# Band attention's q and k: from a token-wise projection inside the mixer stage to four units of seven products ahead of it

## The chip, the cores and the metric

One Trainium2 chip, one core in use. The metric is the device time of one execution in microseconds (us), the median over runs; lower is better. Everything is float32: a product of two float32 matrices is made from fp32r parts, each operand split into a high part (a cast) and a low part (what the cast lost), as three matmuls: high by high, high by low, low by high.

## The reference, cut to what matters

One layer of a streaming encoder for 1024 tokens of width 1024. The part that the change touches is the second of two token mixers, attention in a band:

```python
h = rmsnorm(x, norm_mix_g)
qa, fa, ia, ga, qb, kb, vb, gate_a, gate_b = split(h @ w_in)
oa = hgrn2_mixer(qa, fa, ia, ga, ...)            # 4 heads of 128
qh = head_rms(qb.reshape(8 heads, 64), qn_g)     # norm over the 64 features of a head, times a gain
kh = head_rms(kb.reshape(8 heads, 64), kn_g)
scores = qh . kh * 64 ** -0.5 + bias[clipped distance]     # own chunk of 64 and the 8 before it
ob = softmax(scores) . vb
x = x + (sigmoid(gate_a) * (oa @ w_a) + sigmoid(gate_b) * (ob @ w_b)) @ w_out
x = x + SwiGLU(rmsnorm(x));  x = x + sigmoid(rmsnorm(x) @ w_pg) * (p @ w_pe)
```

`head_rms(t, g)` is `t * rsqrt(mean(t * t) + 1e-6) * g`.

## The kernel before, in words

Activations lie feature by feature: a tile has 128 features on the partitions and 1024 tokens along the free axis. The kernel runs through these stages in order.

**Units of seven products** (`units`, L900). The normed input `u` is eight pairs of tiles. After a first stage come ten jobs (`JOBS`), each of which makes two blocks of 128 output features for all 1024 tokens. A job is one call of `strassen` (L1605): the 2 x 2 block product (two feature blocks by two token halves) is made with seven products instead of eight, each product being 4 x 3 matmuls of 128x128 by 128x512, so 84 matmuls a unit. Sums of weight quarters, their casts and low parts are made one unit ahead (`strassen_weights`: DVE sums, ACT casts, POOL and DVE low parts), in steps called `side` between the products. DVE adds products together; each finished quarter (block `c`, token half `half`) goes to a callback `done`. A "gate" or "out" unit's callback, `gate_done` (L888), multiplies by the row of the outer norm (`rb`), applies a sigmoid or silu, and stores the 128x512 result to DRAM. Temporaries of 128x512 come from a pool of eight (`stmp`, tag "tmp"). PSUM has eight banks of 128x512; a unit uses three.

**HGRN mixer** (`hgrn_mix`). Four heads, woven with a filling stream of matmul pieces (`fill`): gates, the projection of v (`attn_v`), and the first four pieces of the next stream, `feed`.

**Attention** (`attention`, L722). 32 steps, each a (pair of heads, block of 128 tokens). `feed` begins with `attn_in` (L609): the q/k projection token by token, in two passes of eight blocks of four pieces (a piece is six matmuls); for each block ACT squares, DVE sums over 64 columns, POOL takes the power -1/2, and DVE scales and doubles the columns. For each step `attn_stack` (L646) transposes four 128x128 blocks on TensorE and writes the stacks to which scores are computed: for q, 64 rows of high part over 64 rows of low part; for k, the high part twice (`k1`) and the low part twice (`k2`), so that two matmuls make a score block. After `attn_in`, `feed` holds the last two gate blocks (`gate`), eight pieces each. Two pieces of `feed` are put into every step.

A step n, in the order in which each engine gets its work: last stage of head 1 of step n-1 (reciprocal and scaling of its probabilities), scores of step n for head 0 and head 1 (matmuls, then on DVE `tensor_tensor_reduce`: add the bias and keep the running minimum of the negated scores), on odd steps the probability-times-v products of the two steps n-3 and n-2, the transposes of step n-1 for head 1 (`attn_pt`, copies by ACT and DVE), exponentials of head 0 and head 1 on ACT with their sums, transposes of step n-1 for head 0, scaling of head 0. A block has 128 to 640 key columns: the first four blocks of a pair have fewer. The steps go through the blocks with two pairs side by side.

The order on TensorE, DVE, ACT, POOL and the DMA queue of SP is pinned: `Pinned` and `order` (L88) chain each instruction to the one before it on its engine, so an engine works in the order of the program. In the profile, L72 is that helper for DVE, ACT and POOL, L102 is `mul`, L105 is `tr`, L97 is `load`; tiles have to be told apart by name (`pm` PSUM, `s` a slot of 128x1024, `m` a small tile of the mixer, `t` a temporary, `whi`/`wlo`/`wh`/`wl` weight parts, `wr` raw weights, `q` weight sums, `d` DRAM).

**The rest.** Branch products, output projection, 22 feed-forward units of seven products, the down projection and the last block. The sums of weight quarters for two of these are made by DMA: `copies` in the mixer, then adding transfers on POOL's queue (`adds`), one every other step of the attention loop, the others later.

Of the kernel before, what the change touches and what calls it, by code (L numbers as in the profile page):

```python
# [10 lines left out]
F32 = mybir.dt.float32  # L11
# [20 lines left out]
FIRST = 4  # L32
RING = 4
# [4 lines left out]
JOBS = (('gate', 6), ('head', 1), ('gate', 8), ('head', 2), ('gate', 10), ('head', 3), ('gate', 12), ('gate', 14), ('out', 0), ('out', 2))  # L38
# [36 lines left out]
class Trunk:  # L75
    def __init__(self, tc, d, out):
# [5 lines left out]
        self.queue, self.calls = None, 0  # L82
        self.by_turns = self.pinned = False
# [162 lines left out]
    def norm_sums(self):  # L246
# [9 lines left out]
        if self.epsv is None:  # L256
            self.epsv = self.small(8, tag="epsv")
            nc.vector.tensor_scalar(self.epsv, v, EPS, None, ALU.mult)
# [12 lines left out]
    def setup(self):  # L271
# [6 lines left out]
        one = cp.tile([P, 3], F32, name="ones")  # L278
        self.ones, self.warm, self.gq8 = [one[:, i:i + 1] for i in range(3)]
        nc.vector.memset(self.ones, 1.0)  # L280
        nc.vector.tensor_copy(self.onesr, self.ones[:, :].to_broadcast([P, P]))
# [3 lines left out]
        nc.vector.tensor_scalar(self.gq8, self.cols[:, C_GQ:C_GQ + 1], 0.125, None, ALU.mult)  # L285

# [136 lines left out]
    def hgrn_mix(self, h):  # L423
# [26 lines left out]
        while m < P:  # L450
# [46 lines left out]
            if m == 16:  # L497
                self.keep_heads(self.oa, self.od, self.done_heads)
            yield 1240
# [14 lines left out]
        if self.oa[h] is None:  # L514
            self.oa[h] = self.slot()
        pks = []
# [87 lines left out]
    def attn_setup(self):  # L604
        self.k1 = [self.slot(F32R) for _ in range(4)]
        self.k2 = [self.slot(F32R, late=i > 1) for i in range(4)]
        self.qs = {}

    def attn_in(self):  # L609

        nc = self.nc
        late = []

        def scale():
            two, b, ps, ss = late.pop(0)
            for i in range(2):
                qk = self.small(HALF, tag="qk")
                self.V.tensor_tensor(
                    qk[:, :].rearrange("p (a two d) -> p a two d", two=2, d=64),
                    ps[:, i * 256:i * 256 + 256].rearrange("p (a d) -> p a d", d=64).unsqueeze(2).to_broadcast([P, 4, 2, 64]),  # L620
                    ss[:, 4 * i:4 * i + 4].unsqueeze(2).unsqueeze(3).to_broadcast([P, 4, 2, 64]), ALU.mult)
                self.qk[2 * two + i, b] = qk

        for two in range(2):
            ws = self.weights(4, ahead=0)
            for b in range(8):
                pss = []
                for n, _ in enumerate(self.tokens(ws, (b,), pss)):
                    if b == 7:
                        self.weights(0, ahead=n + 1 if two == 0 else 2, direct=True)  # L630
                    if n < 3:
                        yield 1296
                    if n == 0 and late:
                        scale()
                (ps,) = pss
                sq = self.small(HALF, tag="sq")
                self.A.activation(sq, ps, AF.Square)
                ss = self.small(8)
                self.V.tensor_reduce(ss, sq[:, :].rearrange("p (a d) -> p a d", d=64), axis=AX.X, op=ALU.add)
                self.V.tensor_scalar(ss, ss, 1.0 / 64, self.epsv[:, b:b + 1], ALU.mult, ALU.add)  # L640
                self.G.tensor_tensor(ss, ss, self.mhalf[:, 0:8], ALU.pow)
                late.append((two, b, ps, ss))
                yield 1296
        self.scale = scale

    def attn_stack(self, pair, b):  # L646

        qk = self.qk.pop((pair, b))
# [1601 lines left out]
```

## Time and profile before

| | before |
|---|---|
| median of 3 runs | 1546.96 us (1546.4 to 1548.36) |
| the profiled execution | 1549.86 us, span 1548.0 us |
| granted TensorE clock | 1.00 |
| TensorE busy | 1520.7 us (98%) |
| VectorE (DVE) busy | 1127.2 us (73%) |
| ScalarE (ACT) busy | 670.7 us (43%) |
| GpSimd (POOL) busy | 626.7 us (40%) |
| one unit of seven products | 19.02 us |
| attention loop, first score matmul to last probability-times-v | 434.6 to 633.5 us |

How to read the lines: a row of a table by stretch gives the stretch, its length, and for each engine busy time with the number of instructions, then the granted clock, the DMA share and the rate. A row of a group gives line, engine, operation, output<-inputs, shapes and count, then busy time and mean duration in ns, then the idle time of that engine just before these instructions and what ended it. A row in order of time gives start, duration, engine, line and operation, and in brackets the idle time before it. PE is TensorE, PEld its weight load. Durations of matmuls overlap, since they are pipelined; from start to start is what one costs in a stream.

### The profile page before, as it was taken

How to read it: one execution, taken by the hardware profiler on the slowest of the kernel's cores; microseconds unless marked ns; L12 is line 12 of the kernel's file. 1: busy time of each engine (PE TensorE's matmuls, PEld its weight loads, DVE VectorE, ACT ScalarE, POOL GpSimd, SP SyncE). 2: the span in 40 equal slices, each digit the busy share in tenths (PEclk: the TensorE clock that was granted, in tenths of full speed). 3: DMA queues.
4: the chain of work that ended last, by engine and by line, in shares of the span. 5: the costliest groups of instructions: out<-in, count | busy, mean ns of one | idle time of the engine just before them, and what ended most of it. 6: DMA issues, size and time to landing. Idle time of an engine off the chain costs nothing.

```text
span 1548.0 us, 20662 instructions
## 1 busy us (share of the span) xinstructions
PE 1520.7 (98%) x7664; PEld 1266.2 (82%) x7664; DVE 1127.2 (73%) x1645; ACT 670.7 (43%) x1136; POOL 626.7 (40%) x349
## 2 busy tenths in 40 slices
PE   8999999999999999999999999999999999999998
PEld 6888888878788888788888788888888888888886
DVE  5787774776777778446888877777777767656678
ACT  6633333433377677421567222222222234456552
POOL 4233333010333222245212656665555545445546
PEclk9999999999999999999999999999999999999999
DMA  5544444898433443767346244443233288785425
GB/s 201 195 164 143 143 150 154 270 325 258 145 82 69 111 75 73 294 178 230 102 158 216 91 119 125 128 124 111 104 110 101 101 303 305 273 282 188 130 96 203
DMA packets 97044, 256.56 MB, mean 166 GB/s; under 512 B 10032, under 2 KB 14896, under 8 KB 96432
## 3 DMA queue, kind: packets, MB, share of 16 engines
q1 hardware_dynamic: 90400, 239.51, 45.0%
q0 software_dynamic: 6400, 15.73, 6.2%
q8 instruction: 60, 0.98, 0.3%
q14 instruction: 40, 0.33, 0.1%
q10 hardware_dynamic: 144, 0.02, 0.0%
HBM read 193.08 MB, written 93.59 MB: 185 GB/s over the span
## 4 chain that ended last, share of the span: by engine, by line
PE 89%; DVE 6%; ACT 2%; DMA 1%; issue 1%; POOL 0%; SPq 0%; DVEq 0%; ACTq 0%; POOLq 0%
PE pm L102 86%; DVE s L72 4%; PE pm L105 3%; DVE m L72 1%; ACT m L72 0%; ACT wh L142 0%; DMA s<-in_x 0%; DMA wr<-in_qk 0%; DMA wr<-in_fm 0%; DVE q L72 0%; ACT s L72 0%; DVE wl L72 0%; DMA wr<-in_wv 0%; DVE s L337 0%; DVE t L72 0%
## 5 line engine op out<-in xcount | busy, mean ns | idle before, releaser
L102 PE MATMUL pm<-s,whi 128*128 128x512 f32 x1792 | 552.4, 389 | 0.6 <-DVE t L72 0.6
L102 PE MATMUL pm<-s,wh 128*128 128x512 f32 (+1 forms) x1584 | 492.5, 392 | 7.0 <-ACT wh L142 5.2
L102 PEld LDWEIGHTS pm<-s,whi 128*128 128x128 f32 x1792 | 336.0, 188 | 71.5 <-DVE t L72 1.7
L102 PEld LDWEIGHTS pm<-s,wh 128*128 128x128 f32 x1584 | 295.6, 188 | 69.9 <-ACT wh L142 5.2
L102 PE MATMUL pm<-s,wlo 128*128 128x512 f32 x896 | 348.6, 389 | 0.0
L72 DVE TENSOR_TENSOR s<-s,s 128x512 f32<-128x512 f32 (+3 forms) x236 | 285.5, 1238 | 61.2 <-ACT s L72 47.7
L102 PE MATMUL pm<-s,wl 128*128 128x512 f32 x792 | 308.7, 390 | 0.5 <-POOL wl L150 0.5
L150 POOL TENSOR_TENSOR wl<-wr,wh 128x1024 fp32r<-128x1024 f32 (+2 forms) x72 | 175.3, 2440 | 222.5 <-ACT wh L142 222.4
L72 DVE TENSOR_TENSOR t<-pm,t 128x512 f32<-128x512 f32 x158 | 108.8, 689 | 132.9 <-PE pm L102 105.6
L142 ACT CAST wh<-wr 128x1024 fp32r<-128x1024 f32 (+2 forms) x106 | 106.5, 1005 | 208.4 <-PE pm L102 92.1
L102 PEld LDWEIGHTS pm<-s,wlo 128*128 128x128 f32 x896 | 168.2, 188 | 34.8
L102 PE MATMUL pm<-wh,s 128*128 128x512 f32 x512 | 180.0, 407 | 0.0
L102 PEld LDWEIGHTS pm<-s,wl 128*128 128x128 f32 x792 | 149.2, 188 | 32.0 <-POOL wl L150 1.2
L72 POOL TENSOR_TENSOR wlo<-wr,whi 128x512 fp32r<-128x512 f32 (+1 forms) x63 | 132.3, 2106 | 68.2 <-ACT whi L72 59.2
L72 POOL TENSOR_TENSOR wlo<-q,whi 128x512 fp32r<-128x512 f32 x62 | 100.0, 1614 | 139.7 <-ACT whi L72 75.5
L72 POOL TENSOR_TENSOR m<-m,mhalf 128x8 f32<-128x8 f32 (+1 forms) x24 | 35.0, 1459 | 229.1 <-DVE m L72 229.1
L72 ACT CAST s<-s 128x1024 fp32r<-128x1024 f32 (+1 forms) x94 | 90.4, 981 | 61.9 <-DVE s L72 31.6
L72 ACT CAST whi<-q 128x512 fp32r<-128x512 f32 (+1 forms) x93 | 70.5, 758 | 107.3 <-PE pm L102 84.6
L102 PEld LDWEIGHTS pm<-wh,s 128*128 128x128 f32 x512 | 96.4, 188 | 18.5
L72 POOL TENSOR_TENSOR s<-t,rb 128x512 f32<-128x512 f32 x44 | 70.7, 1607 | 98.5 <-ACT t L72 96.1
L102 PE MATMUL pm<-wl,s 128*128 128x512 f32 x256 | 99.9, 390 | 0.0
L72 ACT ACTIVATE t<-s 128x512 f32<-128x512 f32 x44 | 27.8, 633 | 159.3 <-DVE s L72 155.3
(147 smaller groups left out, 1835.3 us busy)
## 6 DMA issues: line engine op xcount, KB each, us to landing
s<-d SPq DMA_DIRECT2D x81, 512.0 KB, 6.2
d<-s SPq DMA_DIRECT2D x87, 256.0 KB, 2.4
wr<-d SPq DMA_DIRECT2D x36, 512.0 KB, 3.7
d<-s SPq DMA_DIRECT2D x32, 512.0 KB, 4.4
d<-t SPq DMA_DIRECT2D x46, 256.0 KB, 2.3
wr<-in_sg SPq DMA_DIRECT2D x22, 512.0 KB, 3.9
wr<-in_su SPq DMA_DIRECT2D x22, 512.0 KB, 4.9
s<-in_x SPq DMA_DIRECT2D x21, 512.0 KB, 8.6
```

The costliest lines, as they stand in the source:

```text
L72: return lambda *a, **k: self.trunk.order(op(*a, **k), self.key)
L102: return self.order(self.nc.tensor.matmul(*a, **k))
L105: return self.order(self.nc.tensor.transpose(*a, **k))
L142: self.nc.scalar.copy(hi[:, c], raw[:, c])
L150: rest.tensor_tensor(lo[:, c], raw[:, c], f32(hi[:, c]), ALU.subtract)
```

## The change

- q and k of pair p (128 features each) become the two blocks of a new kind of unit, `("qk", p)`. Four of them are put among the last jobs, so there are fourteen units. Units q/k 0 and 1 stand between gate and out units, 2 and 3 stand side by side, and one out unit follows.
- Their callback `qk_done` works on 128x512: multiply by `rb` (DVE), square (ACT), cast to a high part (ACT), low part (DVE). From then on the rest of the chain is done one step per product (`tick`), beginning two products later: two matmuls with a constant block matrix `blk` (1/64 inside each head's 64 x 64 block) sum over partitions; logarithm with eps as bias, then exponential of -1/2 of it (ACT); multiply (DVE); scale by the gain into a high part (ACT); low part (DVE); store both parts to DRAM (`qkd`).
- The attention stage loads q and k back as stacks: `attn_q` loads for each head 64 rows of the high part over 64 rows of the low part, 512 tokens at a time; `attn_k` loads the high part twice and the low part twice. For the first pair this is asked for in head 3 of the HGRN mixer, for later pairs in blocks 4 and 5 of the pair before, the bias in block 6.
- `attn_in`, `attn_stack`, their eight weight tiles and `epsv` go. `feed` is the two gate blocks alone; three pieces are used ahead of the attention loop, one in each of the steps 4, 8, 12, 16, 20, 24 (`FILL`), the rest after it.
- The steps go through one pair after the other. Score tiles `s` have four buffers instead of three.
- Adding transfers are issued in every fourth step instead of every second one. Heads of the result are stored at other steps.

```diff
-JOBS = (('gate', 6), ('head', 1), ('gate', 8), ('head', 2), ('gate', 10), ('head', 3), ('gate', 12), ('gate', 14), ('out', 0), ('out', 2))
+FILL = (4, 8, 12, 16, 20, 24)
+JOBS = (
+    ('gate', 6), ('head', 1), ('gate', 8), ('head', 2), ('gate', 10), ('head', 3), ('gate', 12), ('qk', 0), ('gate', 14), ('qk', 1),
+    ('out', 0), ('qk', 2), ('qk', 3), ('out', 2))
...
+        nc.vector.tensor_scalar(self.blk, f32(self.onesr[:, :]), 0.0, None, ALU.mult)
+        for r in (slice(0, 64), slice(64, P)):
+            nc.vector.tensor_scalar(self.blk[r, r], f32(self.onesr[r, r]), 1.0 / 64, None, ALU.mult)
...
+    def attn_q(self, p, half):
+        hs = slice(half * HALF, half * HALF + HALF)
+        for h in range(2):
+            q = self.q[p, h, half] = self.small(HALF, F32R, tag="qk")
+            for i in range(2):
+                self.load(f32(q[64 * i:64 * i + 64, :]), self.qkd[p][0][i][64 * h:64 * h + 64, hs])
+
+    def attn_k(self, p, h):
+        self.k[p, h] = [self.slot(F32R) for _ in range(2)]
+        for k, src in zip(self.k[p, h], self.qkd[p][1]):
+            for i in range(2):
+                self.load(f32(k[64 * i:64 * i + 64, :]), src[64 * h:64 * h + 64, :])
...
-        steps = [(2 * two + p, b) for two in range(2) for b in range(8) for p in range(2)]
+        steps = [(p, b) for p in range(4) for b in range(8)]
-        feed = chain(self.feed, self.gate(ahead=3), self.gate(ahead=2))
+        feed = self.feed
...
+        def loads(p, b):
+            if b == 0:
+                self.attn_q(p, 1)
+            if p < 3 and b == 4:
+                self.attn_q(p + 1, 0)
+            if p < 3 and 4 <= b < 6:
+                self.attn_k(p + 1, b - 4)
+            if p < 3 and b == 6:
+                self.attn_bias(p + 1)
...
-            if n % 2 and n < whole:
+            if n % 4 == 1 and n < whole:
                 next(self.adds)
             stage(n - 1, 1)
-            next(feed, None)
+            if n in FILL:
+                next(feed, None)
             if n < whole:
...
                 scores(n, 0)
-            st = stack(n + 1)
-            next(st, None)
-            if n < whole:
                 scores(n, 1)
-            drain(st)
+                loads(*steps[n])
             if n % 2:
                 pv(n - 3)
                 pv(n - 2)
             pt(n - 1, 1)
-            next(feed, None)
             stage(n, 0)
             stage(n, 1)
             pt(n - 1, 0)
             stage(n, 0)
...
+    def qk_done(self, p, t, c, half, ps):
+        ...
+        sq, hi, lo = self.stmp(), self.stmp(F32R), self.stmp(F32R)
+        V.tensor_tensor(t, ps, self.rb[:, hs], ALU.mult)
+        A.activation(sq, t, AF.Square)
+        A.copy(hi, sq)
+        V.tensor_tensor(lo, sq, f32(hi), ALU.subtract)
+
+        def steps():
+            ps = self.mm()
+            self.mul(ps, self.blk, hi, start=True, stop=False)
+            self.mul(ps, self.blk, lo, start=False, stop=True)
+            yield
+            r = self.stmp()
+            A.activation(r, ps, AF.Ln, bias=self.eps[:, 0:1])
+            A.activation(r, r, AF.Exp, scale=-0.5)
+            yield
+            V.tensor_tensor(t, t, r, ALU.mult)
+            yield
+            h = self.stmp(F32R)
+            A.activation(h, t, AF.Copy, scale=g)
+            yield
+            V.scalar_tensor_tensor(t.bitcast(F32R), t, g, f32(h), ALU.mult, ALU.subtract)
+            yield
+            for to, src in zip(self.qkd[p][c], (h, t)):
+                self.store(to[:, hs], f32(src))
+
+        self.due.append([2, steps()])
+
+    def tick(self):
+        for job in list(self.due):
+            job[0] -= 1
+            if job[0] <= 0 and next(job[1], self) is self:
+                self.due.remove(job)
...
-SMALL = {"rb": 1, "rtok": 1, "epsv": 1, "t8": 2, "t4": 4, "mx2": 4, "den": 4}
+SMALL = {"rb": 1, "rtok": 1, "t8": 2, "t4": 4, "mx2": 4, "den": 4}
-MIXER = {"s": 3, "pt": 4, "bias": 4, "qk": 4, "qs": 2, "sq": 1, "state": 2}
+MIXER = {"s": 4, "pt": 4, "bias": 4, "qk": 4, "state": 2}
```

More of the change, by code (lines that the diff above doesn't have):

```diff
@@ L907, in units @@
         self.hd = [[] for _ in range(4)]
+        self.qkd = [[[self.spill() for i in range(2)] for c in range(2)] for p in range(4)]
         self.kept = []
@@ L2069, in run @@
                 self.load(self.masks, d["masks"])
-                self.feed = self.attn_in()
+                self.feed = chain(self.gate(ahead=3), self.gate(ahead=2))
+                self.q, self.k = {}, {}
                 fill = chain(*[self.gate_first(c) for c in FIRSTS], self.attn_v(), islice(self.feed, FIRST))
```

137 lines of the change are left out of this document (41 added, 96 removed).

## The prediction, made before the changed kernel ran

> **What bounds the kernel now.** I read the engine sums and the chain first, then busy time by stretch, then the groups and the order of time inside the attention loop and inside one seven-product unit.
>
> ```profile
> PE 1520.7 (98%) x7664; PEld 1266.2 (82%) x7664; DVE 1127.2 (73%) x1645; ACT 670.7 (43%) x1136; POOL 626.7 (40%) x349
> PE 89%; DVE 6%; ACT 2%; DMA 1%; issue 1%; POOL 0%; SPq 0%; DVEq 0%; ACTq 0%; POOLq 0%
> core 0: us, PE busy (x) PEld busy (x) DVE busy (x) ACT busy (x) POOL busy (x), PEclk, DMA share, GB/s
> 218.63:237.65 19.02, 19.02 (x86) 15.75 (x85) 11.83 (x14) 6.58 (x11) 6.51 (x5) 1.00 0.47 151
> 426.10:434.60 8.50, 8.50 (x46) 6.96 (x45) 4.51 (x11) 4.38 (x13) 2.95 (x3) 1.00 0.00 0
> 434.60:633.50 198.90, 192.79 (x1450) 167.32 (x1449) 155.49 (x504) 141.91 (x372) 55.98 (x38) 1.00 0.40 92
> ```
>
> TensorE is 98% busy and carries 89% of the chain. The first stretch is one whole unit of seven products (84 matmuls in 19.02 us, 0.226 us each); VectorE has 7 us to spare in it. The last is the attention loop, from its first score matmul to its last probability-times-v: 198.9 us, TensorE idle for 6.1. A saved TensorE microsecond is therefore a saved microsecond only while TensorE remains the last to finish. In that loop the covering work is exactly what is taken out:
>
> ```profile
> L102 PE MATMUL pm<-wh,s 128*128 128x512 f32 x221 | 81.8, 414 | 0.0
> L102 PE MATMUL pm<-wl,s 128*128 128x512 f32 x110 | 43.0, 391 | 0.0
> 573.28 0.47 PE L102 MATMUL pm<-wh,s 128*128 128x512 f32 x1
> 574.75 0.60 PE L105 MATMUL pm<-eye,m 128*128 128x128 f32 x4
> 575.10 0.48 PE L102 MATMUL pm<-wh,s 128*128 128x512 f32 x1
> ```
>
> 331 recorded matmuls of the loop are the token-wise q/k projection. One piece of six takes 573.28 to 574.75, 1.47 us; the four transposes of one stack take 574.75 to 575.10, 0.35 us.
>
> **The change, part by part.** *TensorE work.* Out go 64 pieces of q/k projection (two passes, eight blocks, four pieces): 64 x 1.47 = 94.1 us; and 32 stacks of four transposes: 32 x 0.35 = 11.2 us. In come four units, 4 x 19.02 = 76.1, and 16 norms of two matmuls, 32 x 0.226 = 7.2: together 83.3 us. (A unit's weight casts and low parts on ACT, POOL and DVE are inside its row; those of the eight old q/k weight tiles leave the loop and the stage ahead of it, where they held TensorE only within the 6.1 us.) On TensorE alone the change is worth 83.3 - 105.3 = -22 us. What it truly gives is this, plus the TensorE idle time that it opens in two places.
>
> *The attention loop.* Before, it held 68 pieces (56 of q/k, 12 of the two gates); after, the six that FILL names. TensorE's own work falls to 192.8 - 62 x 1.47 - 11.2 = 90.5 us. Less work on ACT and DVE too, but a closed ring remains, step after step: reciprocal of head 1's denominator, its scaling, the two bias-and-minimum scans of head 0, the two of head 1, head 1's exponential with its sum, then the next reciprocal. The program fixes that order on DVE, so no step can be shorter than the ring. These rows are its links at full width (640 columns):
>
> ```profile
> 617.82 0.15 DVE L72 RECIPROCAL m<-m 128x1 f32<-128x1 f32 x1
> 618.01 0.55 DVE L72 TENSOR_SCALAR m<-m,m 128x640 f32<-128x640 f32 x1
> 618.48 0.55 DVE L72 CUSTOM_DVE_ANT_0 m<-pm,m 128x384 f32<-128x384 f32 x1
> ...
> 572.32 0.55 DVE L72 CUSTOM_DVE_ANT_0 m<-pm,m 128x384 f32<-128x384 f32 x1
> 573.57 0.56 DVE L72 CUSTOM_DVE_ANT_0 m<-pm,m 128x384 f32<-128x384 f32 x1
> 574.76 0.83 ACT L72 ACTIVATE m<-m,m 128x640 f32<-128x640 f32 x1
> 575.50 0.19 ACT L72 ACTIVATION_READ_ACCUMULATOR m<-m,m 128x1 f32 x1
> ```
>
> Reciprocal to first scan 0.66 (617.82 to 618.48), head 0's scans 1.25 (572.32 to 573.57), head 1's scans to its exponential 1.19, the exponential to the end of its sum 0.93 (574.76 to 575.69), hand-over 0.1: 4.13 us. Four of a pair's eight steps are this wide. The other four have 512, 384, 256 and 128 columns:
>
> ```profile
> L72 DVE CUSTOM_DVE_ANT_0 m<-pm,m 128x384 f32<-128x384 f32 x40 | 22.1, 553 | 16.8 <-PE pm L105 16.7
> L72 DVE CUSTOM_DVE_ANT_0 m<-pm,m 128x256 f32<-128x256 f32 x16 | 6.7, 421 | 5.1 <-PE pm L105 5.1
> L72 DVE CUSTOM_DVE_ANT_0 m<-pm,m 128x128 f32<-128x128 f32 x8 | 2.2, 286 | 3.7 <-PE pm L105 3.7
> L72 ACT ACTIVATE m<-m,m 128x640 f32<-128x640 f32 x48 | 39.9, 832 | 9.6 <-DVE m L72 9.3
> L72 ACT ACTIVATE m<-m,m 128x384 f32<-128x384 f32 x12 | 7.4, 620 | 1.7 <-DVE m L72 1.7
> L72 ACT ACTIVATE m<-m,m 128x128 f32<-128x128 f32 x12 | 4.8, 400 | 2.0 <-DVE m L72 1.9
> 617.98 2.40 PE L102 MATMUL pm<-m,s 128*64 128x128 f32 x40
> 627.16 0.74 PE L105 MATMUL pm<-eye,m 128*128 128x128 f32 x5 [2.76 <-DVE m L72]
> ```
>
> With their shorter scans and exponentials, and only one scan a head up to 384 columns, I estimate 3.7, 2.8, 2.3 and 1.9. A pair takes 4 x 4.13 + 10.7 = 27.2, four pairs 109 us. The DVE idle times of these rows (25.5 us until transposes) are the score tile's three buffers: head 1's scan waits until the step before is transposed. A fourth buffer removes that wait, and the ring is late next. On top come 3 us for odd steps, where two blocks of probability-times-v (2.40 us) stand ahead of the transposes that ACT's copies need before the exponentials; 7 us of DVE work that sits in the ring (gate products and low parts of weights, about ten of 0.7); and 6 us at the end, where the last transposes at 627.16 are followed by the last product's end at 633.5 with nothing to cover it. Loop: 125 us; 34 of them are TensorE idle, against 6 before. It begins about 3 us earlier, with one piece and one stack fewer ahead (the 8.50 us stretch). Gain 198.9 - 125 + 3 = 77. Bounds: ring and drain alone, 115, gain 87; and 1.2 us lost in each of 16 odd steps instead of 3 in all, 141, gain 61. I take 77, near the ring, because its links are measured.
>
> *The four units.* A gate unit's DVE time is 11.83 of 19.02 us. Each of a q/k unit's four halves keeps the gate's product with rb and adds three DVE operations (low part of the square, product with the norm, low part of the result), and DVE itself must wait, in its order, while ACT squares and casts:
>
> ```profile
> L72 DVE TENSOR_TENSOR t<-t,t 128x512 f32<-128x512 f32 x2 | 1.4, 693 | 0.2
> L72 DVE SCALAR_TENSOR_TENSOR s<-t,cols,s 128x512 fp32r<-128x512 f32 x2 | 1.4, 744 | 0.0
> L72 ACT ACTIVATE t<-t 128x512 f32<-128x512 f32 x28 | 17.7, 633 | 76.8 <-DVE t L72 67.9 <-issue 8.5
> L72 ACT CAST s<-t 128x512 fp32r<-128x512 f32 x4 | 2.4, 622 | 0.9 <-DVE t L72 0.9
> 188.76 0.55 DVE L72 TENSOR_SCALAR s<-s,lb,lb 128x512 f32<-128x512 f32 x1 [0.70 <-ACT s L72]
> 162.10 0.68 DVE L72 TENSOR_TENSOR q<-wr 128x512 f32<-128x512 f32 x1
> 238.26 2.64 DVE L72 TENSOR_TENSOR q<-wr 128x512 f32<-128x512 f32 x1
> 237.95 2.40 POOL L72 TENSOR_TENSOR wlo<-wr,whi 128x1024 fp32r<-128x1024 f32 x1 [0.51 <-ACT whi L72]
> ```
>
> Work: 4 x (0.69 + 0.69 + 0.74) = 8.5, so 20.3 us. Waits: the head units show 0.70 for one ACT operation between two of DVE (188.76); two in a row make about 1.3, four times 5.2. So DVE is taken for 25.5 us where TensorE needs 19.02 + 8 x 0.226 = 20.8. The excess is 4.7 us a unit, 19 in all. Behind the waiting DVE stand the additions that free PSUM banks (the fourth product of a unit cannot enter its bank before DVE has read it) and the low part of the square that TensorE needs two products later. About half of each chain falls into the unit that follows; after q/k units 0 and 1 this is a gate or silu unit with 7 us free, but units 2 and 3 are adjacent. Worked through in order, I get about 2.5 us of TensorE wait behind each of the first two and 8 behind the last two: 13. Bounds: 0, if the neighbours' 7 us take it all; and 28, the whole 19 and 9 more where POOL keeps DVE out (the same operation took 0.68, and 2.64 while POOL's ran at 237.95). I take 13.
>
> ACT's load in such a unit is 6.58 - 2.5 + 4 x about 3.2 (square, cast, logarithm, exponential, scaled copy) = 16.9 of 20.8, so it is not the bound. Table loads: the order of the jobs changes function set five more times if logarithm and exponential share one:
>
> ```profile
> L72 ACT ACT_TABLE_LOAD x7 | 9.0, 1283 | 9.7 <-issue 7.4 <-DVE s L72 2.2
> d<-t SPq DMA_DIRECT2D x46, 256.0 KB, 2.3
> DMA to landing us min/median/max: 2.8/7.4/8.0
> ```
>
> 5 x 1.28 = 6.4 us of ACT, in its slack: nothing. The Trainium skill's page "ScalarE: Activation LUTs", section "Table sets: the hidden batching unit", says that a set with both functions exists; by that rule it stays at five. No run here shows which set is chosen for this pair, so the other case is a rival below.
>
> *Costed at nothing, with the cover.* The 32 stores (2.3 us each to landing, no one waits, but the eight temporaries of a unit come back only then; this is inside the 28) and 64 half-height loads run on SP, where DMA share is 0.40. The next pair's k and q loads are issued three to four steps ahead, 12 us or more; its two 320 KB bias loads two steps ahead, 8 us, as long as the slowest took (8.0, the third row above), and SP, free by then, may issue them sooner. Eight sum transfers move from the loop's POOL queue to the feed-forward units, where one is issued a unit. The constants at the start and the dropped epsv fall where TensorE has no idle time from them.
>
> **Sum.** 83.3 + 13 - 77 = +19. The profiled execution took 1549.9 us (span 1548.0), so 1569; the median, 1547.0, is 2.9 below it: **1566 us**. The forecast's own range is 1550 to 1590.
>
> **The rivals.** *TensorE stays the bound* (faster, 0.18): the ring overlaps better than I think and the units' DVE excess is absorbed. Full price -22, 1525 us. It decides once the newly opened TensorE idle is under 22 us; I count 28 + 13 = 41. For it: VectorE has 43 us of slack in the loop before. Against: that slack is counted beside 68 cover pieces. Halfway, a loop of 116 and 5 us in the units, it ends within 0.2% (0.10); 0.2%, 3 us, is about what a measurement of this kernel can tell from no change.
>
> *Tables swap in every half* (0.06): logarithm and exponential in different sets, 32 more loads, 41 us of ACT. A q/k unit then needs 16.9 + 10.3 = 27.2 us of ACT, 6.4 over TensorE: +26, 1592 us.
>
> *Reloads come late* (0.04): stacks or bias not there at a pair's first step, three switches of up to 8 us: +24, 1590 us. Against: 8 to 12 us of lead.
>
> **How the numbers follow.** Forecast 0.62; with the two heavier rivals, slower 0.72; same 0.10; faster 0.18. The range reaches from 1541, a little into the faster case, to 1592, the upper prices: outside lie most of the 0.18 and little above.
>
> **What would show it.** The loop (first to last scan) near 118 us, TensorE busy there 70 to 75%, DVE's waits now on ACT's exponentials instead of transposes; a score step at full width of 4.1 to 4.6 us. In the units: fourteen instead of ten, q/k units of 21 to 27 us, TensorE's idle released by DVE (low part of the square, PSUM reads); five more table loads, not 37. It is wrong if full steps run under 3.8 us, or the units add less than 86.

## The result, and the profile after

1611.43 us median (1608.14 to 1613.12, four runs) against 1546.92: 4.1% slower, ratio 1.0413, 95% interval 1.0394 to 1.0431. The forecast was slower, at 1566 us; it is 45 us short, and above the range's upper end of 1592.

Engine sums and the chain of the changed kernel:

```profile
PE 1538.3 (95%) x7520; PEld 1264.1 (78%) x7520; DVE 1137.4 (71%) x1588; ACT 734.7 (46%) x1154; POOL 610.8 (38%) x343
PE 80%; ACT 8%; DVE 7%; issue 3%; DMA 2%; SPq 0%; POOL 0%; DVEq 0%; ACTq 0%; POOLq 0%
```

Its stretches: the units from 218 us (before the first q/k unit's norm) to their end; HGRN to the first score matmul; the attention loop; all that follows:

```profile
218.00:401.08 183.08, 153.82 (x601) 119.88 (x600) 113.72 (x137) 126.75 (x163) 42.94 (x26) 0.92 0.33 115
401.08:565.65 164.57, 156.56 (x1011) 131.31 (x1010) 117.67 (x208) 64.56 (x138) 22.43 (x14) 0.99 0.79 251
565.65:693.62 127.97, 106.34 (x968) 91.66 (x966) 90.97 (x352) 100.93 (x261) 8.80 (x8) 0.96 0.64 160
693.62:1605.34 911.72, 909.66 (x4018) 748.30 (x4018) 650.89 (x683) 347.17 (x459) 455.84 (x248) 1.00 0.54 173
```

The same three last stretches of the kernel before:

```profile
270.04:434.60 164.56, 158.25 (x1027) 132.79 (x1026) 120.76 (x215) 65.97 (x142) 23.44 (x15) 1.00 0.73 236
434.60:633.57 198.97, 192.86 (x1450) 167.39 (x1449) 155.49 (x504) 141.91 (x372) 55.98 (x38) 1.00 0.40 92
633.57:1542.03 908.46, 905.80 (x4030) 749.51 (x4030) 657.82 (x688) 350.32 (x463) 449.92 (x240) 1.00 0.52 170
```

The units end 401.08 - 270.04 = 131.0 us later; the forecast had 96.3. HGRN is as long as before (forecast: 3 shorter). The loop is 71.0 us shorter (forecast 73.9). The rest is 3.3 us longer (forecast 0). So 35 of the 45 us were lost in the units. There TensorE stands idle for 183.08 - 153.82 = 29 us, ACT is busy for 126.75 us, and the granted clock is 0.92. A group of the page:

```profile
L75 ACT ACT_TABLE_LOAD x41 | 52.6, 1283 | 3.0 <-DVE s L75 2.2
```

The largest waits in that stretch (us in total, times, longest):

```profile
DVE t L75 <- ACT t L75: 28.3, 16, 4.2
PE pm L106 <- DVE t L75: 26.0, 10, 5.3
DVE s L75 <- ACT t L75: 24.2, 14, 3.2
```

41 table loads instead of 7: one ahead of every logarithm and every exponential of the norm. The first row of waits is the low part of the square, which waits for square and cast; the third is the product with the norm, which waits for the exponential. In order of time, one such place:

```profile
250.74 1.28 ACT L75 ACT_TABLE_LOAD   x1
252.03 0.69 ACT L75 ACTIVATE t<-pm,ones 128x512 f32<-128x512 f32 x1
252.74 1.28 ACT L75 ACT_TABLE_LOAD   x1
254.03 0.63 ACT L75 ACTIVATE t<-t 128x512 f32<-128x512 f32 x1
254.69 0.69 DVE L75 TENSOR_TENSOR s<-s,t 128x512 f32<-128x512 f32 x1 [2.68 <-ACT t L75]
255.30 0.68 DVE L75 TENSOR_TENSOR t<-pm,t 128x512 f32<-128x512 f32 x1
256.04 1.22 PE L106 MATMUL pm<-s,whi 128*128 128x512 f32 x2 [5.28 <-DVE t L75]
```

And the stretch just after it:

```profile
256.10:261.30 5.20, 5.20 (x12) 4.12 (x13) 4.60 (x5) 3.68 (x6) 3.23 (x2) 0.50 0.24 89
```

Load, logarithm, load, exponential; DVE waits 2.68 us; behind its product in its order stands the addition that frees a PSUM bank; TensorE stands for 5.28 us. In the last row TensorE is busy, but at half clock (0.50). The Trainium skill, page "TensorE: Matmul & The Clock Gate", section "Part 1: The HAM clock gate (the "warmup" mystery)", has the clock fall to half after an idle window of about 3.4 us; that agrees with this row. As a least length of a stall it is not borne out: in the same stretch the clock was also 0.50 from 377.85 to 381.10, after a stall of 2.89 us, and in run 1 below after one of 1.97 us.

### The profile page after: what moved, and what is told of

Its sections match the earlier page's. It is cut to its first block, busy times and chain, and to the rows that moved or that the text cites. A ratio compares the mean times of both kernels' runs of the same rounds, so it can differ in the third digit from the quotient of the medians.

```text
span 1611.3 us, 20543 instructions
## 1 busy us (share of the span) xinstructions
PE 1538.3 (95%) x7520; PEld 1264.1 (78%) x7520; DVE 1137.4 (71%) x1588; ACT 734.7 (46%) x1154; POOL 610.8 (38%) x343
## 4 chain that ended last, share of the span: by engine, by line
PE 80%; ACT 8%; DVE 7%; issue 3%; DMA 2%; SPq 0%; POOL 0%; DVEq 0%; ACTq 0%; POOLq 0%
PE pm L106 78%; DVE s L75 4%; ACT t L75 3%; ACT m L75 2%; PE pm L109 2%; ACT L75 1%; DVE m L75 1%; DMA wr<-in_wv 1%; DVE t L75 1%; ACT whi L75 1%; ACT wh L146 0%; DMA wr<-in_fm 0%; DMA s<-in_x 0%; ACT s L75 0%; DVE q L75 0%
## 5 line engine op out<-in xcount | busy, mean ns | idle before, releaser
L106 PE MATMUL pm<-s,whi 128*128 128x512 f32 x2016 | 635.9, 397 | 25.4 <-DVE t L75 25.4
L106 PEld LDWEIGHTS pm<-s,whi 128*128 128x128 f32 x2016 | 383.0, 190 | 114.6 <-DVE t L75 29.1
L106 PE MATMUL pm<-s,wlo 128*128 128x512 f32 x1008 | 398.8, 396 | 0.0
L106 PEld LDWEIGHTS pm<-s,wlo 128*128 128x128 f32 x1008 | 191.7, 190 | 43.7
L75 DVE TENSOR_TENSOR t<-pm,t 128x512 f32<-128x512 f32 x178 | 122.5, 688 | 133.7 <-PE pm L106 121.5
L75 POOL TENSOR_TENSOR wlo<-wr,whi 128x1024 fp32r<-128x1024 f32 (+1 forms) x71 | 148.1, 2092 | 109.2 <-ACT whi L75 100.4
L75 POOL TENSOR_TENSOR wl<-wr,wh 128x1024 fp32r<-128x1024 f32 x14 | 34.5, 2466 | 144.7 <-ACT wh L146 143.7
L106 PE MATMUL pm<-wh,s 128*128 128x512 f32 x256 | 87.1, 404 | 0.0
L75 DVE TENSOR_TENSOR s<-s,pm 128x512 f32<-128x512 f32 x72 | 46.7, 682 | 49.3 <-PE pm L106 49.3
L75 DVE TENSOR_TENSOR s<-pm,s 128x512 f32<-128x512 f32 (+1 forms) x66 | 43.9, 679 | 49.6 <-PE pm L106 46.5
```

The lines of the kernel that those rows point to most:

```text
L75: return lambda *a, **k: self.trunk.order(op(*a, **k), self.key)
L106: return self.order(self.nc.tensor.matmul(*a, **k))
```

## The experiments

Each edit is on the kernel named in its expectation. The kernel before, measured beside each group of runs, took 1546.9 to 1550.2 us, so a difference between runs of two groups is uncertain by about 3 us; the ratios are to the kernel before of the same group. Runs 1 to 4 are one group, 5 to 8 the next, then 9 to 12, 13 to 15, 16 and 17, and 18. Theory at the outset: the table loads made the excess. Rival: DVE's order and its waits, with POOL and the temporaries, made it, and the loads lay in ACT's slack.

**1. One set named by hand.**

```diff
+            if the set last loaded isn't the one with both functions: load it
             A.activation(r, ps, AF.Ln, bias=self.eps[:, 0:1])
             A.activation(r, r, AF.Exp, scale=-0.5)
```

> The norm of q and k keeps its logarithm and exponential, but one table set that holds both is named by hand where the set last loaded was another, so that no load stands between them. Theory T (the 32 table loads made the excess of the units): loads fall from 41 to about 14, the units give back the difference between what they added (+51 beside the TensorE work) and the forecast's 13, so 1611 - 38 = 1573 us (1565 to 1582), TensorE's granted clock in the units back at 0.99 or more, and HGRN ending about 97 us later than before instead of 134. Theory W (DVE's waits for ACT, for POOL and for temporaries made it; the loads lay in ACT's slack): 1598 us or more, HGRN still over 120 us late.

1584.52 us (ratio to before 1.0231, 1.0211 to 1.0251): 26.9 us won. Table loads, then the units' stretch, then its waits:

```profile
L75 ACT ACT_TABLE_LOAD x12 | 15.4, 1283 | 7.8 <-DMA d<-t 5.4 <-DVE s L75 2.2
```

```profile
218.00:376.44 158.44, 144.75 (x608) 113.90 (x606) 116.01 (x138) 89.78 (x135) 44.62 (x27) 0.99 0.38 133
```

```profile
DVE t L75 <- ACT t L75: 23.7, 16, 2.9
PE pm L107 <- DVE t L75: 11.7, 11, 2.0
DVE s L75 <- ACT t L75: 2.2, 5, 0.6
```

12 loads are the 7 of before and the five that the prediction counted for one shared set. DVE's wait for the exponential falls from 24.2 to 2.2 us. The units are 24.6 us shorter: TensorE's idle time falls from 29.3 to 13.7, and its busy time by 9.1 for the same matmuls, which is the half clock; no stall is longer than 2.0 us, and the clock is 0.99. It isn't 1.00 because of one place, behind the longest stall, 1.97 us:

```profile
359.55:363.00 3.45, 3.45 (x10) 2.68 (x9) 3.28 (x5) 2.46 (x5) 0.37 (x1) 0.51 0.21 53
```

The loads are the larger part of the excess. But the units are still 106.4 us longer than before, 23 over TensorE's 83.3, so 11 us of the expectation are missing.

**2. Half the loads: the set loaded ahead of every logarithm.**

```diff
+            A: load the set with both functions, always
             A.activation(r, ps, AF.Ln, bias=self.eps[:, 0:1])
```

> One table load (the set with both functions) before each of the 16 logarithms, none before the exponentials: half the dose. T as a matter of ACT's time: a q/k unit needs 16.9 + 4 x 1.28 = 22.0 us of ACT against 20.8 of TensorE, so nearly all is won back, 1575 to 1585 us. T as a matter of latency (each load delays the norm that TensorE and DVE wait for): half, about 1592 us. W: 1600 or more.

1590.62 us (1.0269, 1.0253 to 1.0284). 25 loads, 13 more than in run 1, cost 6 us; the next 16 cost 21. The price isn't proportional. The stretch:

```profile
218.00:379.91 161.91, 147.33 (x607) 116.01 (x605) 114.13 (x137) 107.41 (x149) 43.85 (x27) 0.97 0.38 133
```

The stretch is 3.5 us longer than in run 1: TensorE's idle time, 14.6 us, is 0.9 of it, the rest is clock, 0.97. The longest stalls here are five of 2.2 to 2.3 us, and the clock was 0.50 behind three of them.

**3. One function for two.**

```diff
-            A.activation(r, ps, AF.Ln, bias=self.eps[:, 0:1])
-            A.activation(r, r, AF.Exp, scale=-0.5)
+            A.activation(r, ps, AF.Abs_reciprocal_sqrt, bias=self.eps[:, 0:1])
```

> Logarithm and exponential replaced by one reciprocal square root, from a set of its own that is loaded only where the function before it was another. T: as the one-set kernel without one ACT operation of 0.7 us a half, 11 us of ACT less: 1565 to 1575 us, of it up to 8 us from shorter waits of DVE. W: 1590 us or more, since DVE's order is unchanged.

1589.97 us (1.0261, 1.0243 to 1.028), 5 above run 1, where 10 to 20 less was expected. 12 loads again, ACT busy for 79.9 us instead of 89.8 in the units, and they end at 377.39, no earlier. (The two profiled executions are only 1.6 us apart; where the 5 us lie is open.) Once the swaps are gone, ACT's time isn't what the units wait for.

**4. Ring of the loop: head 1's scaling moved between the scans.**

```diff
-            stage(n - 1, 1)
                 scores(n, 0)
+                stage(n - 1, 1)
                 scores(n, 1)
```

> The table loads stay as in the changed kernel; in the attention loop head 1's reciprocal and scaling move from ahead of both heads' scans to between head 0's scans and head 1's, so that head 0's scans drop out of the closed ring. Ring theory (the loop of 128 us is set by the ring, 4.6 to 4.9 us a full step): the ring is 1.2 us shorter, DVE's own work of about 4.1 us a full step is late next, the loop takes 118 to 123 us and the time is 1601 to 1606 us. Rival (DVE and ACT queues set the step, not the ring): loop and time unchanged within 3 us; if head 1's later transposes count, some us slower.

1612.63 us (1.0411, 1.0395 to 1.0426): no gain, and the loop from first to last scan is longer, 123.2 against 119.1. Taking head 0's scans out of the ring wasn't enough: DVE's waits for matmuls and transposes rose from 1.5 to 8.2 us, ACT's for the transposes from 10.7 to 17.1. Head 1's transposes come later, and ACT's copies and exponentials behind them. The ring has a second branch of about the same length through them. The expectation of the ring theory, 1601 to 1606 us, failed; its rival's held. Whether the scaling is a link at all is left to runs 6 and 7.

**5. The square straight into its rounded form.**

```diff
-        A.activation(sq, t, AF.Square); A.copy(hi, sq)
-        V.tensor_tensor(lo, sq, f32(hi), ALU.subtract)
+        A.activation(hi, t, AF.Square)
...
-            self.mul(ps, self.blk, lo, start=False, stop=True)
```

> On the one-set kernel (1584.5 us, units 23 us longer than TensorE's added work of 83.3): ACT squares straight into the rounded form, the low part of the square is left out (the norm's mean is taken of the rounded squares). Theory D (DVE's own work and its waits for ACT set the units): DVE's work in a q/k unit falls from 20.3 to 17.5 us and the wait for two ACT operations, 5.2 us a unit, goes; TensorE loses 16 matmuls, 3.6 us. Excess 23 -> about 7: 1565 us (1560 to 1571). Theory P (POOL that keeps DVE out, and temporaries that come back late): little more than the matmuls, 1577 to 1582 us.

1566.21 us (1.0109, 1.0094 to 1.0124), as theory D had it (1565). The stretch and TensorE's wait in it:

```profile
218.00:357.02 139.02, 137.20 (x590) 111.46 (x589) 95.58 (x121) 79.19 (x120) 45.20 (x27) 0.99 0.44 155
```

```profile
PE pm L107 <- DVE t L75: 1.8, 1, 1.8
```

TensorE's idle time is 1.8 us. What was left after the table loads was DVE's work and its waits for the square and the cast. The edit also saves two temporaries a half and so doesn't exclude that they came back late; against it speaks that DVE's waits for stores hardly changed, 5.7 us in run 1 and 4.6 here.

**6 and 7. One link of the ring out, one operation beside it out.**

```diff
 6:  self.V.tensor_scalar(s[:, :cols], s[:, :cols], den, None, ALU.mult)   -> left out
 7:  self.A.activation(s[:, :cols], s[:, :cols], AF.Copy, scale=den)       -> left out
```

> On the one-set kernel: head 1's probabilities are not divided by their sum (DVE's scaling of up to 640 columns, 0.55 us, left out; the reciprocal stays). Ring theory (that scaling is a link of the ring, full steps take 3.97 to 4.4 us): every step shorter by 0.4 to 0.6 us, the loop from 119 to about 106 (first to last scan), time 1571 us (1568 to 1575). Theory A (ACT's queue, 81% busy in the loop, sets the step): DVE's operation was not the limit, 1580 to 1585 us.

> On the one-set kernel: head 0's probabilities are not divided by their sum (ACT's scaled copy of up to 640 columns, about 0.83 us, left out; the reciprocal stays). Ring theory: that copy is no link of the ring, loop and time within 4 us of the one-set kernel, 1580 to 1586 us. Theory A: ACT loses 32 operations of 0.4 to 0.83 us, about 20 us of its 97; the loop falls by 10 to 16 us, to 103 to 109, time 1569 to 1575 us.

The probabilities of the one head are then not divided by their sum; the two kernels serve to find the path and are no versions of the change.

Run 6: 1571.99 us (1.0146, 1.0127 to 1.0166). Run 7: 1588.31 us (1.0246, 1.0231 to 1.0262). First to last scan in the loop, of run 1, run 6 and run 7:

```profile
541.99:661.13 119.14, 99.87 (x906) 85.90 (x906) 87.36 (x345) 96.50 (x252) 8.80 (x8) 0.97 0.68 171
```

```profile
539.25:647.42 108.17, 98.26 (x906) 84.28 (x906) 71.02 (x312) 93.71 (x251) 8.82 (x8) 0.98 0.74 189
```

```profile
538.87:659.64 120.77, 100.48 (x896) 87.33 (x896) 87.59 (x344) 77.87 (x218) 8.92 (x8) 0.94 0.67 169
```

16 us less on DVE, in the ring, make the loop 11.0 us shorter; 19 us less on ACT, the busier engine, beside the ring, make it no shorter. So DVE's scaling lies on the path that sets the loop, and ACT's sum doesn't set it. The scaling stands ahead of head 0's scans and ahead of head 1's transposes; which of the two branches of run 4 is the longer, run 6 doesn't tell.

**8. POOL's low parts of the weights made by DVE.**

```diff
-  more = self.strassen_weights() ...
+  more = self.strassen_weights(self.V if n > 6 else None) ...
```

> On the one-set kernel: from the first q/k unit on, the four low parts of the next unit's weights (POOL, 6.4 us a unit) are made by DVE (3.3 us a unit at 0.68 and 1.2 us). Theory P: DVE's operations that now take 1.7 to 2.9 instead of 0.7 us beside POOL's return to 0.7, 4.8 us a q/k unit by the rows, against 3.3 us of new work: 1577 to 1582 us. Theory D (DVE's own work sets the units): 3.3 us more in four q/k units that have none to spare, 1585 to 1595 us.

1584.91 us (1.0222, 1.0202 to 1.0242), equal to run 1 and between the two theories. DVE's operations do stretch beside POOL's (in run 1 one of 0.75 us took 2.89 while POOL's of 2.51 ran), but giving the work to DVE costs as much. Undecided.

**9, 10 and 12. 32 bytes.** The stretch behind the loop was 3.3 us longer though its TensorE work had not grown (it has one piece of the gates less, and eight sum transfers more), with 2 us of idle time and at clock 1.00. Three matmuls (one with a low part in each three) from start to start, in the changed kernel, in two products of one feed-forward unit:

```profile
1044.43 0.39 PE L106 MATMUL pm<-s,wlo 128*128 128x512 f32 x1
1045.13 0.40 PE L106 MATMUL pm<-s,wlo 128*128 128x512 f32 x1
...
1047.89 0.39 PE L106 MATMUL pm<-s,wlo 128*128 128x512 f32 x1
1048.57 0.39 PE L106 MATMUL pm<-s,wlo 128*128 128x512 f32 x1
```

0.70 and 0.68; before the change it is 0.68 throughout. The slow ones are always the first, fourth and seventh product of a unit: those whose weights lie in half-width tiles. By the addresses in the compiled program these tiles lie 32 bytes past a multiple of 64 in the changed kernel, on a multiple of 64 before. The tiles that moved lie in pools behind `epsv`, 32 bytes, which the change dropped; the full-width weight tiles and the slots lie ahead of it and did not move.

```diff
 9, 10:
-SMALL = {"rb": 1, "rtok": 1, "t8": 2, ...}
+SMALL = {"rb": 1, "rtok": 1, "epsv": 1, "t8": 2, ...}      (and a memset of one such tile)
 12, on the kernel before:
-            self.epsv = self.small(8, tag="epsv")
+            self.epsv = self.small(16, tag="epsv")[:, 0:8]
```

> The changed kernel with its table loads, and nothing but a 32-byte tile put back where the small tile of before (epsv) stood. Theory L (layout: dropping it moved every tile behind it to 32 bytes past a multiple of 64, and matmuls whose stationary operand lies there take 0.698 us for three instead of 0.680): the seven-product units return to 0.680 throughout, 36 units x 12 threes x 0.018 = 7.8 us, and the part of the feed-forward that grew by 6.1 us returns to 728; 1611.4 - 9 = 1602 us (1599 to 1605). Rival (the slower threes come from the sums that now run beside the feed-forward units, or from the clock): 1609 to 1613 us, pattern unchanged.

> The one-set kernel with the square taken straight to its rounded form (1566.2 us) and the same 32 bytes put back. Theory L: 1566.2 - 9 = 1557 us (1554 to 1560). Rival: 1564 to 1568 us.

> The kernel before the change, with nothing but its epsv tile twice as wide (64 bytes for 32), so that the tiles behind it lie at 32 bytes past a multiple of 64, as in the changed kernel. Theory L: 32 units (10 and 22) x 12 x 0.018 = 6.9 us and what the last products add, 1549 + 7 to 9 = 1557 us (1554 to 1559). Rival: no change, 1547 to 1551 us.

Run 9: 1602.97 us (1.0341, 1.0325 to 1.0358), 8.5 less (11 by the ratios). Run 10: 1559.65 us (1.0074, 1.005 to 1.0097), 6.6 less (5 by the ratios). Run 12: 1556.74 us (1.0044, 1.0027 to 1.006), 6.6 more than the kernel before beside it (1550.19). The threes of run 9 and of run 12:

```profile
1043.72 0.39 PE L106 MATMUL pm<-s,wlo 128*128 128x512 f32 x1
1044.40 0.39 PE L106 MATMUL pm<-s,wlo 128*128 128x512 f32 x1
```

```profile
1043.28 0.40 PE L102 MATMUL pm<-s,wlo 128*128 128x512 f32 x1
1043.98 0.40 PE L102 MATMUL pm<-s,wlo 128*128 128x512 f32 x1
```

0.68 and 0.70: the pace goes with the 32 bytes, both ways. That it is the weights' place that counts is read from which products are slow; no run moved the weights alone.

**11, 14 and 15. Products with a scaled identity instead of scaling and transposing.**

```diff
 11:
-            self.A.activation(s, s, AF.Copy, scale=den)  /  self.V.tensor_scalar(s, s, den, ...)
+        self.A.activation(dg, self.eye, AF.Copy, scale=den)                # both heads
-                self.tr(ps[...], s[:, block], self.eye)
+                self.mul(ps[...], s[:, block], dg, start=True, stop=True)
 14:     head 1's dg by self.V.tensor_scalar(dg, self.eye, den, None, ALU.mult)
 15:  FILL = (4, 7, 9, 12, 15, 17, 20, 23, 25);  JOBS end: qk 1, qk 2, qk 3, out 0, out 2
```

Run 11 is on run 10, run 14 on run 11, run 15 on run 14.

> On the kernel before this one: neither head's probabilities are scaled; instead ACT scales the identity by the reciprocal (128 x 128, about 0.3 us), and the transposes become products with that diagonal. DVE's scaling leaves the ring (0.55 us and its gap in a full step), ACT loses head 0's scaled copy of 0.83 us and gains two of 0.3. Ring theory: the loop falls from 119 to 106 to 109 us as it did without head 1's scaling, time 1557 - 12 = 1545 us (1541 to 1549), below the kernel before. Rival (ACT's scaled identity and the hand-over to TensorE take the scaling's place in the ring, or these products are slower than transposes): 1555 us or more.

> On the kernel with the products against a scaled identity (loop 131 us, 1567.8): head 1's scaled identity is made by DVE (128 columns, about 0.2 us, where the scaling took 0.55) instead of behind head 0's on ACT. If the two scaled identities in a row on ACT, ahead of all products and so of ACT's copies and exponentials, lengthened the ring: the loop falls to 110 to 113 us, below the 119.7 without any of this, 1549 to 1552 us. If the products themselves are the slower step: the loop stays over 120 us, 1558 us or more.

> On the kernel before this one: the last three pieces of the gates' projection (4 us of TensorE) move from behind the loop into it, and the last two q/k units stand ahead of both silu units, so that their stores leave before the next stage's loads. Theory: the loop has over 20 us of TensorE idle time to take the pieces, minus 2 to 4 us; the wait for returning temporaries in the last unit (1.8 us, with a slower clock behind it) goes, minus 2 to 3: 1545 us (1541 to 1549), below the kernel before. Rival: a piece in a step costs the ring as much as it saves behind the loop: 1549 to 1553 us.

1567.83 us (1.0116, 1.0097 to 1.0134), 1566.34 (1.0107, 1.0088 to 1.0126) and 1568.4 (1.012, 1.0099 to 1.0142): worse than run 10, as the rivals of runs 11 and 14 had it, and run 15 above both of its expectations. First to last scan of run 11, and its products; then the transposes of the changed kernel's loop:

```profile
514.65:645.62 130.97, 121.37 (x1121) 111.88 (x1122) 73.89 (x313) 95.75 (x281) 8.83 (x8) 0.97 0.61 156
```

```profile
L107 PE MATMUL pm<-m,m 128*128 128x128 f32 x445 | 58.4, 284 | 9.1 <-ACT m L75 9.1
```

```profile
L109 PE MATMUL pm<-eye,m 128*128 128x128 f32 x230 | 33.3, 287 | 16.1 <-DVE m L75 16.1
```

Two matmuls were recorded for a float32 product where a transpose has one; TensorE is busy for 121 of 131 us and near the bound again. These runs say nothing on the ring. Of run 15 the order of the units is worth keeping: they end at 348.70 instead of 351.36 in run 14.

**13. Swaps kept, DVE's product later.**

```diff
             yield
+            yield
             V.tensor_tensor(t, t, r, ALU.mult)
-            yield
             h = self.stmp(F32R); A.activation(h, t, AF.Copy, scale=g)
...
-FFN = {..., "tmp": 8}
+FFN = {..., "tmp": 9}
```

> The changed kernel with all its table loads; in each half of a q/k unit DVE's product with the norm comes one product of the unit (2.7 us) later behind ACT's exponential, and ACT's scaled copy in the same step as it; one more temporary (nine). Theory D (the loads cost by DVE's wait in its order for the exponential, 24.2 us in the units, behind which its additions and TensorE stand): that wait falls below 8 us and the time to 1592 us (1588 to 1597). Theory A (the loads cost by ACT's own time, 27.2 us a unit against 20.8): the work on ACT is the same, 1605 to 1615 us.

1602.28 us (1.034, 1.0319 to 1.0362): between the two. The wait for the exponential fell from 24.2 to 7.3 us as planned, but the waits came back elsewhere:

```profile
DVE t L75 <- ACT t L75: 34.9, 21, 4.2
DVE s L75 <- ACT t L75: 7.3, 6, 3.2
DVE wlo L75 <- ACT whi L75: 7.1, 3, 2.4
```

ACT, late by its loads, now holds DVE at the square (34.9, was 28.3) and at the weights' casts. Both theories carry part of it: about a third of the loads' 27 us (9 by the medians, 11 by the ratios) goes with DVE's place in the order, or with the ninth temporary that the edit needs; the two aren't separated. How the rest divides is open.

**16, 17 and 18. Using the loop's idle TensorE and POOL.** All on run 10 with the units' order of run 15.

```diff
 16: FILL = (4, 7, 9, 12, 15, 17, 20, 23, 25)
 18: FILL = (4, 6, 12, 14, 20, 22, 28, 30)
 17: self.G.tensor_scalar(s[:, :cols], s[:, :cols], den, None, ALU.mult)    # head 1, POOL for DVE
```

> On the kernel with one set, the rounded square and the 32 bytes (1559.7 us, loop 119.7 of which TensorE is busy 100): the last two q/k units stand ahead of both silu units (their first stores then leave 2.7 us earlier by the run before), and the three pieces of the gates' projection that followed the loop (4 us of TensorE) stand in it. Theory: the TensorE idle time of the loop takes the pieces; minus 2.7 and minus 2 to 4: 1554 us (1552 to 1556). Rival (a piece in a step lengthens the ring's step by its own 1.4 us, since the transposes that ACT waits for stand behind it): minus 2.7 alone, 1556 to 1559 us, loop 122 to 124.

> On the kernel with one set, the rounded square and the 32 bytes (1559.7 us): the same order of the units (minus 2.7), and head 1's scaling on POOL, idle for 110 of the loop's 120 us, in place of DVE. Ring theory: DVE's 0.55 us and gap leave the ring, as in the run without that scaling, loop 108 to 112 us, 1547 us (1544 to 1551), about the kernel before. Rival (POOL keeps DVE out while it scales, as its low parts did in the units, or its sums' transfers stand ahead of the scaling in its queue): loop 120 us or more, 1557 us or more.

> On the kernel with one set, the rounded square and the 32 bytes (1559.7 us): the order of the units as in the two runs before (minus 2.7), and eight pieces of the gates' projection in the loop, all in even full-width steps (where a step with a piece took 4.23 us against 4.14), none in a pair's first step (3.5 us with a piece, against an estimated 1.9) and none in an odd step (5.3 to 5.5 with one). Theory (a piece is free where no probability-times-v and no narrow step stands beside it): loop 119.7 less about 1.6 for each of three first steps, plus about 0.3 for each of five more pieces, 115 to 117 us; two pieces fewer behind it, 2.7; 1559.7 - 2.7 - 3 - 2.7 = 1551 us (1548 to 1554). Rival (each piece lengthens its step by its own 1.4 us wherever it stands): loop 122 us, 1557 us or more.

1562.68 us (1.0082, 1.0068 to 1.0097), 1576.6 (1.0176, 1.016 to 1.0193) and 1556.27 (1.0051, 1.0035 to 1.0066). First to last scan of run 10, of run 16, of run 17 with POOL's scaling behind it, and of run 18:

```profile
514.85:634.56 119.71, 99.96 (x900) 86.83 (x901) 87.48 (x344) 96.06 (x250) 8.80 (x8) 0.96 0.67 170
```

```profile
512.51:643.45 130.94, 107.43 (x921) 93.45 (x922) 88.84 (x345) 96.74 (x251) 8.81 (x8) 0.93 0.61 156
```

```profile
510.96:650.81 139.85, 103.50 (x884) 91.61 (x886) 74.19 (x311) 93.00 (x248) 52.14 (x38) 0.91 0.57 146
```

```profile
L75 POOL TENSOR_SCALAR m<-m,m 128x640 f32<-128x640 f32 x15 | 28.3, 1885 | 46.7 <-DVE m L75 25.1 <-PE pm L107 21.6
```

```profile
513.58:637.03 123.45, 104.92 (x918) 90.84 (x918) 87.29 (x345) 96.44 (x252) 8.87 (x8) 0.94 0.64 165
```

Three pieces, with some in odd steps, lengthen the loop by 11 us, more than either expectation of run 16 had (the clock is lower too, 0.93 for 0.96); two more in even steps only, by 4, to 123.5 us, near the 122 of run 18's rival; the time of run 18 lies between its two theories. Idle TensorE time in the loop isn't free. POOL's scaling takes 1.885 us where DVE's took 0.55, and the loop is 20 us longer, as run 17's rival had it. Run 18 has the lowest median of the versions of the change, 0.5% over the kernel before (its interval overlaps that of run 10); none beats it.

## Why the prediction was right or wrong

*The attention loop, -77: right, 6 us short.* 128.0 us for a forecast 125, and the 3 us ahead of it did not come: HGRN took 164.57 us for 164.56 before, though 161.0 in run 5, where the units' waits are gone. First to last scan 119.1 for "near 118"; DVE's waits moved from transposes to ACT's exponentials, as these two rows of the changed kernel show (first to last scan):

```profile
DVE m L75 <- ACT m L75: 22.6, 36, 2.2
DVE m L75 <- PE pm L109: 1.5, 3, 0.5
```

Head 1's reciprocals there, at full width:

```profile
606.33 0.16 DVE L75 RECIPROCAL m<-m 128x1 f32<-128x1 f32 x1 [0.62 <-ACT m L75]
610.23 0.16 DVE L75 RECIPROCAL m<-m 128x1 f32<-128x1 f32 x1 [0.52 <-ACT m L75]
614.37 0.16 DVE L75 RECIPROCAL m<-m 128x1 f32<-128x1 f32 x1 [0.42 <-ACT m L75]
618.33 0.16 DVE L75 RECIPROCAL m<-m 128x1 f32<-128x1 f32 x1 [0.25 <-ACT m L75]
622.89 0.16 DVE L75 RECIPROCAL m<-m 128x1 f32<-128x1 f32 x1 [0.65 <-ACT m L75]
```

Steps of 3.90 (the first with 640 columns), 4.14, 3.96 and 4.56 us, for a ring of 4.13. Two things beside it were off. TensorE was busy there for 106 us (83%) instead of 90.5 (70 to 75%); the lower clock, 0.96, accounts for at most some 5 of the 16 (0.04 of 128), the rest is open. And the ring isn't one chain: run 4 showed the branch through the transposes.

*TensorE's work in the units, +83.3:* confirmed by run 10. Without loads, low part of the square and layout the units end at 352.17, 82.1 us later than before, for 83.3 - 3.6 = 79.7 of work, with 1.9 us idle.

*TensorE's waits in the units, +13: mis-sized, inside its bounds.* Without the loads the excess was 23 us, of which the layout is 5 (357.02 to 352.17 from run 5 to run 10): 18. DVE's wait for square and cast had the forecast size, 23.7 us in 16 waits in run 1, 1.5 each for 1.3, and with it and the operation behind it taken out (run 5) TensorE's idle time fell from 13.7 to 1.8 us. The mechanism was right, the size of what reaches TensorE 5 us too small.

*"Table loads ... in its slack: nothing": the step that failed.* The count of five rested on the rule of the Trainium skill, page "ScalarE: Activation LUTs", section "Table sets: the hidden batching unit": a logarithm and an exponential need one load, since a set has both. Such a set exists, run 1 shows it in use, with 12 loads. But the changed kernel, which names no set, has a load ahead of every logarithm and another ahead of every exponential, 16 times each, 41 in all. The rival "Tables swap in every half" had this mechanism, with a price of 26 us; run 1 won back 26.9. Its chance of 0.06 was the error. Its working, ACT's sum over TensorE's in each q/k unit, is borne out in part. Behind the first q/k unit ACT works for 24.5 us with hardly a gap:

```profile
233.00:257.50 24.50, 17.32 (x71) 13.20 (x70) 15.14 (x19) 24.18 (x29) 4.40 (x3) 0.95 0.20 75
```

For half the loads the same working gives 4 x (22.0 - 20.8) = 5 us, and run 2 cost 6. But run 13 won 9 us with ACT's work unchanged, and 9 of the 25 us in the units are the lower clock, which no step had. That 26 met 26.9 is therefore partly luck.

*"The dropped epsv ... no idle time": wrong as well.* It cost no idle time but 8.5 us of pace (run 9). With the 32 bytes back, in run 10, the stretch behind the loop takes 905.7 us (before: 908.5), and one piece of the gates fewer in it accounts for about half of that difference.

Together: 1566 + 27 (loads) + 8.5 (layout) + 5 (waits) + 3 (loop) = 1609.5, of 1611.4. So close a sum is partly luck: HGRN's missing 3 us and the shorter stretch behind the loop aren't in it, and its terms come from different groups of runs. With the loads cured the time lies inside the forecast's range: 1584.5 in run 1, and without the layout's 8.5 about 1576 (an estimate, no run has only these two). The sign was right in each version.

## What to carry to other kernels

Count the table loads of a planned sequence as if each function came from a set of its own, and when two sets alternate inside a chain that an in-order engine waits for, price the chain, not the busy time. An idle engine beside a closed ring is no free place: ask which link a moved operation stands in front of. When a stretch that nobody touched changes its pace without idle time, compare the addresses of its tiles before looking for a cause in its neighbours.

## What the runs showed of the hardware that was not expected

- Matmuls of 128x128 by 128x512 whose weights lie 32 bytes past a multiple of 64 took 0.70 us for three instead of 0.68; a shift by 32 bytes in both kernels turned it off (8.5 us won) and on (6.6 us lost).
- After a TensorE stall of 5.28 us the granted clock was 0.50 for 5.2 us. Shorter stalls did the same in some places and not in others: behind 1.97 us in run 1 and 1.82 us in run 5 it was 0.50 for over 3 us, behind 1.89 us in run 10 and 1.83 us in the changed kernel (at 296.10) it stayed at 1.00. What decides between them is open.
- Two table sets in turn inside the chain of the norm cost 27 us of 1611 for 32 loads of 1.283 us on ACT, of which 9 us were lower clock on TensorE; 13 loads more than run 1 cost 6 us, the next 16 cost 21.
- POOL's scaling of 128x640 took 1.885 us, DVE's 0.55. A float32 product of 128x128 by 128x128 was recorded as two matmuls, 58.4 us for 445 records; the transposes it replaced, 33.3 for 230.
